# A two-layer encoder trunk on one core: products in couples for nearly all weight panels, with order and memory planned at build time

## Chip, core and metric

The kernel runs on one core of a Trainium2 chip. TensorE (PE) multiplies, VectorE (DVE) and ScalarE (ACT) work element by element, GpSimd (POOL) does small work and issues some DMAs, SyncE (SP) issues the other DMAs. The metric is device microseconds for one execution, as the median of several runs.

## What is computed

The input is 256 rows of 2048 float32 values. Layer 1 is causal softmax attention with 16 heads of 128 and a bias from cumulated forget gates, then a squared-ReLU MLP with 8192 hidden values. From its result come keys and values that layer 2 shares; layer 2 has queries of its own, attention over chunks with a learned bias by distance, and a second MLP. With only 256 rows, the time lies in the products of 256 rows with weights.

```python
h = x
u = rms_norm(h, a_norm_g)
q, k, v, fz = split(u @ a_w_in)                 # 2048 x (3*2048 + 16)
q, k = head_norm(q), head_norm(k)
h = h + forgetting_attention(q, k, v, log_sigmoid(fz + b_f)) @ a_w_out
h = h + relu(rms_norm(h) @ w1[0])**2 @ w2[0]    # 2048 x 8192, 8192 x 2048
k_sh, v_sh = split(rms_norm(h, kv_norm_g) @ kv_w)
q = head_norm(rms_norm(h, b_norm_g) @ b_w_q)
h = h + chunked_relbias_attention(q, head_norm(k_sh), v_sh) @ b_w_out
h = h + relu(rms_norm(h) @ w1[1])**2 @ w2[1]
```

All is float32.

## The kernel before

**Panels and units.** Weights are cut into panels of 512 columns and 2048 rows (16 blocks of 128 rows). There are 96: 12 of `w_in`, 4 of each output projection, 16 up and 16 down of each MLP, 4 of the second query, 8 of `kv`. A panel's weights come in 8 units of two blocks (512 KB). The rows of the result, 256, are two blocks `b`, each with a PSUM bank of its own.

**Three passes.** For precision each operand is split in a high part, rounded to `float32r`, and a low part, the rest. `issue` (L213 on) does it for weights: ScalarE writes `hi` (L227), VectorE `lo` (L228). `passes` (L485 on) then multiplies high by high (L491), low activations by high weights (L493), high activations by low weights (L495). A panel takes 2 x 16 x 3 = 96 matmuls of 512 columns.

**Couples.** Two panels side by side form a pair, and in a pair two row blocks of weights make, with two row blocks of the result, a product of 2 x 2 by 2 x 2 blocks. It is done with seven block products instead of eight (a form of Strassen's method after Winograd). I call such a place a couple: it saves one block product, three matmuls. The weight blocks of a couple are named 11, 12, 21, 22, and the seven left factors are 11, T3 = 22 + 12, T2 = T3 + 11, T1 = 12 + 11, 21, T4 = T2 + 21, and 22. All couples of a pair lie side by side in one tile, so that one instruction makes one factor for all of them. T3 and T2 are sums on VectorE (`make`, L848); T1 and T4 are made by a DMA from GpSimd that adds weights in HBM to a tile in place (`put`, L854), except in the first pair of an MLP, where VectorE makes them. The activations need four sums of blocks, split in high and low as well (`sums`, L287 to L307; tiles `S` and `Sh`). Between the forms ScalarE and VectorE move partial results between PSUM banks (L937, L939, L944, L950, L962).

Pairs with couples are in the MLPs and the second query only: 2 couples in the first up pair of a layer, 3 in the other seven (`WIDE1`), 4 in each of the eight down pairs (`WIDE2`), 2 in each of the two query pairs. The rest of a pair's weights, and all other panels, run as plain units.

**Order.** An MLP goes in four chunks of 2048 hidden values: two up pairs, two down pairs. `Pair.plan` lists forms `f`, `h` and units `a` (first panel) and `b` (second); the last three units of a pair's second panel are left over and run between the first forms of the next pair. Work other than the products is queued by hand in `fill`, a list with one slot for each unit of weights; `run_fill` empties one slot after each. `prepare` starts a pair's weights so many units ahead as the tuple `when` says. Weights come on SP's queue with 4 KB a row (`raw`, four buffers), or 6 or 8 KB for the tiles of couples; split units have three buffers. `keep_order` (L39) fixes the written order on VectorE, ScalarE, TensorE and SP.

**Turns.** Activations must have their columns on the partitions for the next product. `blocks32` (L338 on) transposes blocks of 32 x 32 on VectorE into `z`; then the blocks change places, either by `carry` (L344 to L359), which writes `z` to HBM and reads it back in four DMAs on SP, or by `hop` (L361 to L369), with 16 DMAs from SBUF to SBUF, 8 on SP and 8 on POOL. Only the fourth hidden panel of a chunk uses `hop`.

**Attention.** `attend` gives each head of a group of four its slots: scores, softmax, a `carry` of the probabilities, values. In stage one panels run one after the other, q, k, v of group 0, then of group 1 and so on; in the `kv` stage k and v of each group.

## Time and profile before

| what | us |
| --- | --- |
| median of 3 runs | 2097.28 |
| lowest and highest | 2096.98, 2098.1 |
| the profiled execution's own span | 2090.4 |

The span runs from the first to the last instruction of the profiled execution; the median of the runs counts 6.9 us more around it. Lines of the profile give a source line, an engine, an operation with its tiles (out<-in), a count, busy time and the mean of one in ns, then the engine's idle time before these instructions and what ended it. PEld is the loading of the stationary operand, which runs beside the matmuls. Time stamps are us from the span's start.

### The profile page before, as it was taken

Reading aid. Unit: us, or ns where it says so; the run is one execution under the profiler, and the core shown is the slowest. Engines: PE = TensorE matmul, PEld = TensorE weight load, DVE = VectorE, ACT = ScalarE, POOL = GpSimd, SP = SyncE. Lnnn points to the kernel's source line nnn. Section 1 sums busy time; section 2 is a strip of 40 time slices with the busy share of each in tenths; the row PEclk is TensorE's granted clock in tenths of the full one; section 3 lists DMA queues with packets and bytes.
Section 4 is the critical chain, followed back from the end, with each engine's and each line's share of the span. In section 5 each row is a group of like instructions: output and inputs, shape, how many; then the busy total and the mean of one; then the engine's idle time right before and its main releaser. Section 6 shows DMA issues by size and latency. Waiting matters only on the chain.

```text
span 2090.4 us, 26489 instructions
## 1 busy us (share of the span) xinstructions
PE 2076.3 (99%) x9182; PEld 1709.6 (82%) x9182; DVE 1679.5 (80%) x1972; ACT 1288.4 (62%) x1613; POOL 150.1 (7%) x195
## 2 busy tenths in 40 slices
PE   9999999999999999999999999999999999999999
PEld 7888888878887887887878888888788788878877
DVE  5767666889789889889988577778988897898886
ACT  6544454767567667667776445556765675676674
POOL 1111000001001001001011001000010010010010
PEclk9999999999999999999999999999999999999999
DMA  7777778789689789788878777787987986897885
GB/s 285 248 253 240 232 255 264 250 268 296 232 292 283 241 270 298 231 273 287 280 252 269 233 232 234 247 264 266 294 280 233 284 284 232 291 286 237 274 279 182
DMA packets 176151, 545.14 MB, mean 261 GB/s; under 512 B 37760, under 2 KB 70416, under 8 KB 163728
## 3 DMA queue, kind: packets, MB, share of 16 engines
q1 hardware_dynamic: 163088, 477.31, 64.4%
q0 software_dynamic: 12640, 65.57, 16.2%
q8 instruction: 72, 1.18, 0.2%
q14 instruction: 63, 0.52, 0.1%
q10 hardware_dynamic: 288, 0.57, 0.1%
HBM read 503.49 MB, written 35.68 MB: 258 GB/s over the span
## 4 chain that ended last, share of the span: by engine, by line
PE 86%; DVE 5%; DMA 5%; ACT 2%; issue 2%; SPq 1%; ACTq 0%; DVEq 0%
PE acc L491 22%; PE acc L493 22%; PE acc L495 22%; PE s L495 6%; PE s L491 5%; PE s L493 5%; DVE lo L228 3%; DMA turn<-z 2%; DMA raw<-in_w1sa 1%; ACT hi L227 1%; PE s L635 1%; PE po L665 1%; DVE z L341 1%; DMA raw<-in_w1sb 1%; SPq L357 0%
## 5 line engine op out<-in xcount | busy, mean ns | idle before, releaser
L228 DVE TENSOR_TENSOR lo<-raw,hi 128x1024 fp32r<-128x1024 f32 (+1 forms) x542 | 655.2, 1214 | 189.3 <-ACT hi L227 176.1
L227 ACT ACTIVATE hi<-raw 128x1024 fp32r<-128x1024 f32 (+1 forms) x542 | 569.3, 1053 | 311.3 <-PE acc L493 232.4
L491 PE MATMUL acc<-hi,act 128*128 128x512 f32 x2092 | 580.4, 394 | 1.3 <-ACT hi L227 1.3
L495 PE MATMUL acc<-lo,act 128*128 128x512 f32 x2092 | 571.6, 390 | 0.0
L493 PE MATMUL acc<-hi,act 128*128 128x512 f32 x2092 | 571.0, 389 | 0.1
L493 PEld LDWEIGHTS acc<-hi,act 128*128 128x128 f32 x2092 | 392.7, 188 | 83.0 <-DVE act L321 0.7
L495 PEld LDWEIGHTS acc<-lo,act 128*128 128x128 f32 x2092 | 391.3, 188 | 84.6 <-DVE lo L228 3.4
L491 PEld LDWEIGHTS acc<-hi,act 128*128 128x128 f32 x2092 | 390.5, 188 | 82.0 <-ACT hi L227 3.2
L227 ACT ACTIVATE hi<-w 128x1024 fp32r<-128x1024 f32 x202 | 212.7, 1057 | 93.4 <-PE acc L493 42.9
L228 DVE TENSOR_TENSOR lo<-w,hi 128x1024 fp32r<-128x1024 f32 x202 | 245.5, 1219 | 22.4 <-ACT hi L227 19.1
L228 DVE TENSOR_TENSOR lo<-wT,hi 128x1024 fp32r<-128x1024 f32 x142 | 172.2, 1221 | 60.8 <-ACT hi L227 59.1
L227 ACT ACTIVATE hi<-wT 128x1024 fp32r<-128x1024 f32 x142 | 148.1, 1055 | 74.4 <-PE acc L493 32.2
L495 PE MATMUL s<-lo,act 128*128 128x512 f32 x370 | 102.1, 392 | 6.0 <-DVE lo L228 6.0
L491 PE MATMUL s<-hi,act 128*128 128x512 f32 x370 | 101.1, 390 | 0.0
L493 PE MATMUL s<-hi,act 128*128 128x512 f32 x370 | 100.9, 389 | 0.0
L495 PEld LDWEIGHTS s<-lo,act 128*128 128x128 f32 x370 | 68.7, 188 | 23.8 <-DVE lo L228 10.1
L493 PEld LDWEIGHTS s<-hi,act 128*128 128x128 f32 x370 | 69.5, 188 | 14.4
L491 PEld LDWEIGHTS s<-hi,act 128*128 128x128 f32 x370 | 69.3, 188 | 14.5 <-ACT hi L227 0.3
L848 DVE TENSOR_TENSOR wT<-wT,w 128x1024 f32<-128x1024 f32 (+1 forms) x48 | 66.3, 1381 | 1.6
L668 ACT ACTIVATE act<-po 128x256 fp32r<-128x256 f32 x32 | 12.3, 385 | 88.0 <-PE po L666 88.0
L848 DVE TENSOR_TENSOR wT<-w,w 128x1024 f32<-128x1024 f32 (+1 forms) x48 | 65.5, 1364 | 0.3 <-DMA w<-in_w2fa 0.3
L577 POOL TENSOR_TENSOR ss<-ss,mhalf 128x4 f32<-128x4 f32 x32 | 43.5, 1367 | 271.8 <-DVE ss L576 271.8
(209 smaller groups left out, 1968.8 us busy)
## 6 DMA issues: line engine op xcount, KB each, us to landing
raw<-in_w_in SPq DMA_DIRECT2D x95, 512.0 KB, 4.6
raw<-in_w1sa SPq DMA_DIRECT2D x70, 512.0 KB, 6.4
raw<-in_w1sb SPq DMA_DIRECT2D x70, 512.0 KB, 6.1
w<-in_w2fa SPq DMA_DIRECT2D x32, 1024.0 KB, 7.7
raw<-in_w2sa SPq DMA_DIRECT2D x64, 512.0 KB, 8.0
raw<-in_w_kv SPq DMA_DIRECT2D x64, 512.0 KB, 4.7
w<-in_w2fb SPq DMA_DIRECT2D x32, 1024.0 KB, 7.5
raw<-in_w2sb SPq DMA_DIRECT2D x64, 512.0 KB, 7.3
```

The source lines that it names most:

```text
L227: S.activation(hi[:, c], raw[:, c], AF.Copy)
L228: V.tensor_tensor(lo[:, c], raw[:, c], hi[:, c].bitcast(F32), op=ALU.subtract)
L341: V.transpose(z.rearrange("p (j n b c) -> p b n j c", j=4, n=n, b=nb)[:, b], src.rearrange("p (n j c) -> p n j c", n=n, j=4))
L491: TE.matmul(ps[:, cols], xh, cut(hi, j), start=first, stop=False, **kw)
L493: TE.matmul(ps[:, cols], xl, cut(hi, j), start=False, stop=False, **kw)
L495: TE.matmul(ps[:, cols], xh, cut(lo, j), start=False, stop=last, **kw)
L577: G.tensor_tensor(rn, vv, mhalf, op=ALU.pow)
L635: TE.matmul(s[:, P : 3 * P], q[:, a, P:T], k[:, a], start=True, stop=True)
L665: TE.matmul(po[:, :T], v[:, 0, a * P : (a + 1) * P], pT[:, :2], start=True, stop=False)
L668: S.activation(o[i][:, 0], po[:, :T], AF.Copy)
L848: V.tensor_tensor(d, a, b, op=ALU.add)
```

## The change

The file is written anew around a planner, while the arithmetic of a pair stays.

- **Couples in 47 of 48 pairs.** `pair_list` lists the pairs of all stages. `w_in` is paired too: (q0, k0), (v0, q1), (k1, v1), (q2, k2), (v2, q3), (k3, v3); `kv` as (k, v) of each group; both output projections. Couples: 2 in each pair of `w_in` but the first, which has none, 2 in output projections, query and `kv`, 4 in all pairs of the MLPs. T1 and T4 are made by adding DMAs everywhere.
- **Recorded operations.** Nothing is issued while the code runs through the stages. `K.op` records an operation with its engine, an estimated duration, the cells of 128 columns that it reads and writes, and, for a DMA, the transfer time. Dependencies follow from the cells.
- **Planned order.** `deadlines` goes backward from the products, whose order is fixed, and gives each operation a latest start. `schedule` then runs a simulation of the five engines and the DMA: each engine takes the ready operation with the earliest deadline; TensorE takes ready small work first, else the next product; SP only the first in line. `early` keeps a load or a split from starting more than so many us ahead (22 for weights of the first three blocks, 16 for 21 and units, 9 for splits). The simulated order is then issued, and `order_engines` fixes it on all five engines, POOL's too.
- **Planned memory.** Two arenas in SBUF (71 grains of 256 columns for weights and work, 130 for split operands) are given out during the simulation in grains, which come free when their last reader has ended. PSUM: six banks for panels, two for the rest.
- **One stream of weights.** All weights lie in one array `ws` in the order of use; units come two by two, 1 MB with 8 KB a row; blocks of four couples too have 8 KB a row, blocks of two 4 KB.
- **Turns.** All turns of activations use `hop`; only the probabilities still use `carry`.
- **Smaller.** The gate runs in two passes of 16 matmuls with 256 columns; the halving of the first split and of the last unit is gone.

```diff
-AHEAD = 2
-EARLY = 3
-WIDE = UN + 512
-DEEP = 2 * UN
-WIDE1 = (1, 2, 3, 4, 5, 6, 7)
-WIDE2 = (0, 1, 2, 3, 4, 5, 6, 7)
+CELL = 128
+GRAIN = 256
+ROOM = {"sb": 71, "op": 130}
+MM = 0.22667
+NAMES = ("11", "T3", "T2", "T1", "21", "T4", "22")
+
+IN_C, OUT_C, UP_C, DOWN_C, Q_C, KV_C = 2, 2, (4, 4), (4, 4), 2, 2
+
+def orders(c):
+    m = 8 - c
+    keep = min(3, m)
+    a = [("a", u) for u in range(c, 8)]
+    b = [("b", u) for u in range(c, 8)]
+    tail, b = b[m - keep :], b[: m - keep]
...
+    F = [("f", i) for i in range(7)]
+    plan = [F[0], "r", F[1], "r", F[2], "r", F[3]]
+    left = []
+    for i in range(m):
+        left += a[i : i + 1] + b[i : i + 1]
...
+    cuts = {2: (1, 1, 1), 3: (1, 1, 1), 4: (1, 1, 1), 5: (1, 1, 1), 6: (1, 1, 0)}[c]
+    for i, k in enumerate(cuts):
+        plan += left[at : at + k] + [F[4 + i]]
+        at += k
+    return plan + left[at:], tail
...
+    def deadlines(self, start=11.0, margin=1.0):
+        for o in reversed(self.ops):
+            if o.main:
+                o.ls = o.nominal + start
+                continue
+            ls = 1e9 if o.due is None else o.due
+            for s in o.succ:
+                ls = min(ls, s.ls - (0 if s.eng == o.eng and not o.xfer else self.AFTER[o.eng]) - (margin if s.main else 0.0))
+            o.ls = ls - self.cost(o)
...
+                busy[e] = now + o.dur
+                if o.xfer:
+                    dma = max(now + o.dur + 1.8, dma) + o.xfer
+                    o.end = dma + 1.3
+                    heapq.heappush(events, (now + o.dur, 1, -1, "wake"))
+                else:
+                    o.end = now + o.dur
...
+def dv(n):
+    return 0.07 + 0.00104 * n
...
+    def load(buf, a, b, off, w, at, early, q="Y"):
+        eng = {"Y": SY, "S": S}[q]
+        op(q, 0.45, lambda: eng.dma_start(buf.ap(a, b), flat(off, w, at, at + b - a)), w=[(buf, a, b)],
+           xfer=xfer(P * (b - a) * 4, (b - a) * 4), early=early, name="load")
+
+    def plus(buf, a, b, off, w, at):
+        op("G", 0.87, lambda: G.dma_start(buf.ap(a, b), flat(off, w, at, at + b - a), accum_op=ALU.add),
+           r=[(buf, a, b)], w=[(buf, a, b)], xfer=2.0 * P * (b - a) * 4 / 0.39e6, name="plus")
+
+    def split(buf, a, b, early=9.0):
+        hi, lo = opd("hi", b - a), opd("lo", b - a)
+        op("S", da(b - a), lambda: S.activation(hi.f(), buf.ap(a, b), AF.Copy), r=[(buf, a, b)], w=[hi], early=early, name="hi", hold=[lo])
+        op("V", dv(b - a), lambda: V.tensor_tensor(lo.f(), buf.ap(a, b), hi.ap(), op=ALU.subtract), r=[(buf, a, b), hi], w=[lo], name="lo")
+        return (hi, 0), (lo, 0)
...
+                for b, i in ((b12, "12"), (b22, "22"), (b11, "11")):
+                    load(b, 0, w, *self.src[i], 0, 22)
+                self.form[0] = [split(b11, a, b) for a, b in cuts]
...
+                add(bt, b22, b12, "T3")
+                self.form[1] = [split(bt, a, b) for a, b in cuts]
+                add(bt, bt, b11, "T2")
+                if self.adds:
+                    for a, b in cuts:
+                        plus(b12, a, b, *self.src["11"], a)
...
+                self.form[2] = [split(bt, a, b) for a, b in cuts]
+                self.form[3] = [split(b12, a, b) for a, b in cuts]
+                load(b21, 0, w, *self.src["21"], 0, 16)
+                if self.adds > 1:
+                    self.form[4] = [split(b21, a, b) for a, b in cuts]
+                    for a, b in cuts:
+                        plus(bt, a, b, *self.src["21"], a)
...
+                self.form[5] = [split(bt, a, b) for a, b in cuts]
+                self.form[6] = [split(b22, a, b) for a, b in cuts]
+            for j, (off, us) in enumerate(self.loads):
+                raw = Buf("raw", UN * len(us))
...
+                    load(raw, 0, UN * len(us), off, UN * len(us), 0, 16)
+                for i, u in enumerate(us):
+                    self.unit[u] = split(raw, i * UN, i * UN + UN)
...
+        op("Y", 3.4, lambda: go(SY, 0), r=[z], w=[dst], group=tag, xfer=1.0, name="hop")
+        op("G", 4.0, lambda: go(G, 1), r=[z], w=[dst], group=tag, xfer=1.0, name="hop")
...
+    order = K.schedule()
+    for o_ in order:
+        o_.fn()
+    order_engines(tc, (V.engine, S.engine, TE.engine, SY.engine, G.engine))
```

1773 lines of the change are left out of this document (913 added, 860 removed).

## The prediction

> **What bounds the kernel now.** I read the page first: span, share of each engine, clock, chain.
>
> ```profile
> span 2090.4 us, 26489 instructions
> PE 2076.3 (99%) x9182; PEld 1709.6 (82%) x9182; DVE 1679.5 (80%) x1972; ACT 1288.4 (62%) x1613; POOL 150.1 (7%) x195
> PEclk9999999999999999999999999999999999999999
> PE 86%; DVE 5%; DMA 5%; ACT 2%; issue 2%; SPq 1%; ACTq 0%; DVEq 0%
> ```
>
> TensorE is busy for 99% and makes up 86% of the chain. Busy time of pipelined matmuls is not work at full rate, so next comes the timeline of TensorE: the first product, and two units of weights one after the other in the first stage.
>
> ```profile
> 7.39 1.22 PE L491 MATMUL acc<-hi,act 128*128 128x512 f32 x2 [1.28 <-ACT hi L227]
> ...
> 17.15 1.07 PE L491 MATMUL acc<-hi,act 128*128 128x512 f32 x4
> ...
> 19.87 1.07 PE L491 MATMUL acc<-hi,act 128*128 128x512 f32 x4
> ```
>
> A unit is 12 matmuls of 512 columns and takes 19.87 - 17.15 = 2.72 us, 0.2267 us each; this pitch is the price of a matmul here. The work is 96 panels of 96 matmuls; a couple saves one product of three matmuls. From the code before: up pairs 2 + 7 x 3 = 23 couples a layer, down pairs 8 x 4 = 32, the query 2 x 2, so 2 x 55 + 4 = 114. That leaves 9216 - 342 = 8874 matmuls, 2011.4 us. (With warming, gate, heads, small ones and the six that are halved it gives the page's 9182.)
>
> The attention heads come on top; the timeline in the second attention stage:
>
> ```profile
> 1204.40 1.27 PE L491 MATMUL acc<-hi,act 128*128 128x512 f32 x4
> ...
> 1212.77 0.59 PE L665 MATMUL po<-pbuf,v 128*128 128x256 f32 x2
> ...
> 1213.42 0.39 PE L634 MATMUL s<-k,q 128*128 128x128 f32 x2
> ...
> 1213.89 1.28 PE L491 MATMUL acc<-hi,act 128*128 128x512 f32 x4
> ```
>
> Between the two L491 rows lie three units (8.16 us) and the products of one head: 9.49 - 8.16 = 1.33 us, 42.6 us for 32 heads. The gate's 16 matmuls are 3.6 us, the rest some 0.7: 46.9 in all. And the end:
>
> ```profile
> 2085.82 0.40 PE L495 MATMUL acc<-lo,act 128*128 128x256 f32 x2
> ...
> 2086.26 0.88 DVE L613 SCALAR_TENSOR_TENSOR h<-acc,qn,h 128x256 f32<-128x256 f32 x2 [0.68 <-PE acc L495]
> ```
>
> TensorE ends at 2086.2, 4.2 us before the span does. So 7.4 + 2011.4 + 46.9 + 4.2 = 2069.9, and 20.5 us of the span are TensorE waiting. 1.6 of them lie at the start (36 matmuls from 7.39 to 17.15, 9.76 us against 8.16). Where are the others? Windows over one chunk of the first MLP, and over the second attention stage:
>
> ```profile
> 612.00:779.00 167.00, 166.06 (x730) 136.13 (x729) 142.42 (x145) 107.99 (x121) 10.89 (x16) 1.00 0.84 268
> ...
> 1195.00:1380.00 185.00, 185.00 (x850) 154.46 (x849) 131.44 (x231) 90.04 (x149) 11.49 (x12) 1.00 0.74 239
> ```
>
> Columns: window, length, busy us and count of PE, PEld, DVE, ACT, POOL, clock, DMA share, GB/s. At the pitch 167 us hold 736.7 matmuls; 730 ran: 1.5 us lost in a chunk. The attention stage loses nothing. The chain and TensorE's timeline show the chunk's loss, where the up pairs give way to the down pairs:
>
> ```profile
> 601.47 7.60 DMA turn<-z
> ...
> 611.54 7.46 DMA raw<-in_w1sa
> 619.11 1.06 ACT hi L227
> ...
> 629.59 0.73 PE L495 MATMUL s<-lo,act 128*128 128x512 f32 x2 [0.88 <-DVE lo L228]
> ```
>
> SP sits behind the round trip through HBM, issues the weights after it, and some 10 us later TensorE waits for a low half from VectorE. **TensorE's stream is the bound, with 20 us of gaps.** The span stands 6.9 us below the median of 2097.28.
>
> **What the couples take away.** Counted from the new list of 48 pairs: in 5 x 2, out 4 x 2, up and down 32 x 4, query 2 x 2, kv 4 x 2: 10 + 8 + 128 + 4 + 8 = 158 couples. 44 more remove 132 matmuls, 132 x 0.2267 = **29.9 us**, and leave 8742, 1981.5 us. All lie in the stream, so all count as long as nothing else is late.
>
> The Trainium skill, "TensorE: Matmul & The Clock Gate", Back-to-back issue gap, gives about 131 ns sustained for such a load-and-multiply pair and 215.7 ns isolated; by these the saving would be 17.3 or 28.5 us. The trace's pitch in full stretches is 226.7 ns, so the measured price stands.
>
> **What they add on VectorE and ScalarE.** Groups of the lines view (busy us, mean ns), and one back-to-back pair of the timeline:
>
> ```profile
> L228 DVE TENSOR_TENSOR lo<-raw,hi 128x1024 fp32r<-128x1024 f32 x538 | 652.6, 1218 | 188.3 <-ACT hi L227 175.1 <-PE acc L493 9.3 <-PE s L493 0.7
> L228 DVE TENSOR_TENSOR loh<-w,hih 128x512 fp32r<-128x512 f32 x56 | 38.5, 687 | 8.6 <-ACT hih L227 8.5
> L848 DVE TENSOR_TENSOR wT<-wT,w 128x1024 f32<-128x1024 f32 x34 | 41.7, 1225 | 1.2
> L848 DVE TENSOR_TENSOR wT<-wT,w 128x1536 f32<-128x1536 f32 x14 | 24.6, 1759 | 0.5
> L939 DVE SCALAR_TENSOR_TENSOR acc<-s,p 128x512 f32<-128x512 f32 x17 | 11.8, 695 | 0.0
> L296 DVE TENSOR_TENSOR sum<-q 128x256 f32<-128x256 f32 x16 | 6.7, 419 | 0.0
> L227 ACT ACTIVATE hi<-raw 128x1024 fp32r<-128x1024 f32 x538 | 567.0, 1056 | 310.4 <-PE acc L493 232.4 <-PE s L493 31.6 <-DMA raw<-in_w_in 13.5
> ...
> 614.84 2.35 DVE L228 TENSOR_TENSOR lo<-raw,hi 128x1024 fp32r<-128x1024 f32 x2
> ```
>
> - Splits: a pair with c couples splits 16384 + 1536c columns (seven forms of 512c, 8 - c units of 1024 in either panel). In tiles of 1024 that is 939 before and 1005 after; with the 98 halves of before at 0.687, VectorE gains 1005 x 1.218 - 1147 = 77 us, ScalarE 66 x 1.056 = 70.
> - Sums of weights (T3, T2): 1024 columns a couple, 158 x 1.225 = 193 against 142 before: 51 us. T1 and T4 now always come by an adding DMA.
> - Moves between banks: 47 pairs with couples instead of 34, 13 x 2 x 0.695 = 18 us; ScalarE 23.
> - Sums of activations: 25 sets instead of 21, some 10 us (a set is 4 x 0.419 + 1.218).
>
> VectorE: 1679.5 + 156 = 1836 us, 89% of 2055; ScalarE some 67%. In an MLP chunk VectorE has 142.4 of 167 us now; it gets 2.5 for splits (88 tiles against 78 and 14 halves) and 2.7 for sums, 148 of 4 x 180 x 0.2267 = 163.2, or 90%. The pair above begins its second tile 1.13 us after the first, so these busy times overcount a little. I cost all of it at nothing: TensorE covers it. Without cover, in a chunk where VectorE lags by a tile at each boundary, it would be 1.2 us a chunk, within the 1.5 below.
>
> **Turning through hops.** All 60 turns of activations (24 panels outside the MLPs' hidden ones, 32 hidden, 4 between the layers) now go straight from SBUF to SBUF, 8 DMAs on SP and 8 on POOL. Before, only the last panel of each hidden chunk does; the trace of one:
>
> ```profile
> 646.47 1.31 DVE L341 STREAM_TRANSPOSE z<-acc 128x512 f32<-128x512 f32 x2
> ...
> 647.81 5.38 SPq L367 DMA_DIRECT2D q<-z  x8
> ...
> 657.52 1.04 ACT L871 ACTIVATE q<-q 128x1024 f32<-128x1024 f32 x1
> ...
> 661.58 1.23 DVE L882 TENSOR_TENSOR act<-q,act 128x1024 fp32r<-128x1024 f32 x1 [0.82 <-ACT q L878]
> ```
>
> From the block transposes to the finished low half are 16.3 us. In the new order the third hidden panel is wanted at unit a4 of the down pair, behind four forms of c = 4 and three left-over units, 7 x 2.72 = 19 us after the up pair ends. It fits by 2.7 us. The price is 60 x 5.4 = 323 us of SP, in which no weights are issued; weights are planned 16 to 22 us ahead, which hides a hop if the arena has room. Per chunk I take 0.5 us lost, between nothing and the 1.5 of now; eight chunks, 4 us.
>
> **Last heads before the output projection.** k and v of group 3 now end in one pair: k at its end, v three units into the next. That pair wants heads 12 and 13 at a6: seven forms of 1.36, three left-over units and seven own, 36.7 us after k; heads 14 and 15 at a7, 39.4. Turning k needs the norm and the hop, some 16 us by the rows above and this one (two of them):
>
> ```profile
> L577 POOL TENSOR_TENSOR ss<-ss,mhalf 128x4 f32<-128x4 f32 x32 | 43.5, 1367 | 271.8 <-DVE ss L576 271.8
> ...
> 309.25 0.38 PE L634 MATMUL s<-k,q 128*128 128x128 f32 x2
> ...
> 334.15 0.38 PE L666 MATMUL po<-pbuf,v 128*128 128x128 f32 x2
> ```
>
> The last head of stage one takes 24.9 us from scores to values, paced by fill slots of one unit. With heads some 3 us apart that gives 16 + 9 + 25 = 50, 10 us late; without slots there is no lateness. I take 4, nearer to no slots since nothing there is slotted any more; bounds 0 and 10, twice.
>
> **Start, end, DMA.** The first split isn't halved any more: 0.5 us on the 1.6. The last unit is no longer cut by rows, so 0.75 us of residual is added to the 4.2. The DMA queues:
>
> ```profile
> q1 hardware_dynamic: 163088, 477.31, 64.4%
> q0 software_dynamic: 12640, 65.57, 16.2%
> ```
>
> That is 2.82 and 5.16 us of 16 engines per MB. Adding DMAs grow from 110 couples to 158 of 0.524 MB, 25 MB or 130 us; hops instead of round trips save about 27 MB, 77 us, and 8 KB rows some more. The share goes from 81% to at most 84%. I cost it at nothing; loads issued ahead hide it.
>
> **The sum.** 7.4 + 1981.5 + 46.9 + 4.9 = 2040.7, plus waits of 2.1 + 8 + 4 = 14.1: a span of 2054.8, and with the 6.9 around it **2062 us**. So the time is 2047.6 + S with S the waits; S = 49.7 eats everything.
>
> **Rivals.**
> - All hidden: S under 5, about 2050. For it: deep prefetch, an arena in place of three split buffers. Against: a turn that fits by 2.7 us.
> - The plan is late: both head boundaries at 10, chunks at 1.5, so S = 2.1 + 20 + 12 = 34, 2082; with VectorE a tile late as well up to 2093. For it: VectorE at 90% and all five engines in one fixed order, which can't go round a late operation.
> - SP's queue becomes the bound (slower): a hop waits at SP's head for late transposes, and the weights behind it stay unissued, as behind the round trip at 601. If each of the 32 hidden hops costs the 1.5 us that a chunk loses now, 48 more: 2110. It decides from 39 / 32 = 1.2 us a hop. Against it: the hop at 647 delayed nothing that TensorE waited for.
> - POOL's issues are held up by VectorE (slower): 480 hop issues instead of 64. If each waits one tile of 1.2 us, a hop is 8 x 1.2 = 10 us later, the third hidden panel misses a4 by 7 us, 8 times: 2062 + 56 = 2118. Against it, the source view of L367:
>
> ```profile
> L367 POOL DMA_DIRECT2D q<-z x64: 498/498/554, 481.6 to 2019.5; - x64
> ```
>
>   All 64 took 498 to 554 ns beside a VectorE that was 85% busy. The Trainium skill, "SBUF — State Buffer", Who interferes with whom, says that a VectorE operation on two SBUF inputs and a GpSimd operation that reads SBUF lock each other out; by the row, issuing isn't hit.
> - It does not do what it says: TensorE isn't the bound, and fewer products change nothing (within 0.2%). The Trainium skill, "Perfetto Trace Analysis", Identifying the Most-Contended Engine, judges TensorE by its weight loads, 82% here, which would leave 18% room. Against it: the weight load
>
> ```profile
> L493 PEld LDWEIGHTS acc<-hi,act 128*128 128x128 f32 x2092 | 392.7, 188 | 83.0 <-DVE act L321 0.7
> ```
>
>   takes 188 ns of a pitch of 227, 83%, in stretches that wait for nothing: 82% is full here.
>
> **Chances.** Forecast (2053 to 2078) 0.56; all hidden 0.10; late plan (2078 to 2093) 0.14; within 0.2%, which is about what a measurement of this kernel tells from no change, 0.05 (2093 to 2101.5; 0.02 of it the last rival); SP's queue 0.12; POOL 0.03. Faster 0.80, same 0.05, slower 0.15. The range is 2048 to 2093, the first three cases.
>
> **What would show it.** 9060 matmuls in place of 9182 (132 fewer products, 16 more for a gate in two passes, 6 halves fewer). VectorE near 1836 us. In an MLP window of 167 us over 730 matmuls: chunks are better than now. TensorE waiting for values or act of the last heads some 40 us into an output projection: that term. Long SP waits on z with late raw tiles: SP's queue. POOL hop issues over 0.6 us: the lock. I am wrong if TensorE's idle time is well above 35 us, or if the pitch of 0.2267 changes.

## The result, and the profile after

| | before | after |
|---|---|---|
| median of the runs, us | 2097.13 (2093.11 to 2098.1, 4 runs) | 2108.2 (2106.89 to 2110.73, 4 runs) |
| ratio, 95% interval | 1 | 1.0056 (1.0042 to 1.007) |
| profiled execution: span, us | 2090.4 | 2107.1 (its time 2108.88) |
| mean granted clock of TensorE | 1.000 | 0.992 |

The change makes the kernel 0.56% slower. I had forecast 2062 us, 1.7% faster. The page of the changed kernel, span, busy times and DMA queues:

```profile
span 2107.1 us, 27585 instructions
PE 2056.4 (98%) x9060; PEld 1695.7 (80%) x9060; DVE 1804.9 (86%) x2062; ACT 1364.1 (65%) x1658; POOL 438.6 (21%) x701
q1 hardware_dynamic: 108608, 436.93, 56.1%
q0 software_dynamic: 39296, 103.88, 25.3%
```

TensorE runs the 9060 matmuls that were forecast and is busy for 19.9 us less, but the span is 16.7 us longer: TensorE waits more. Which wait? TensorE's list of waits, first the kernel before (waiting line, what released it, total us, times, longest):

```profile
PE s L495 <- DVE lo L228: 7.0, 10, 0.9
PE acc L491 <- ACT hi L227: 1.3, 1, 1.3
PE pt L92 <- DVE mhalf L94: 1.1, 1, 1.1
```

and the changed one:

```profile
PE ps L489 <- ACT ps L574: 18.1, 10, 5.0
PE ps L489 <- ACT arena_op L469: 10.6, 3, 7.6
PE ps L836 <- DMA arena_sb<-arena_sb: 4.6, 2, 2.5
PE ps L491 <- DVE arena_op L1081: 3.8, 3, 2.5
PE ps L869 <- DMA arena_sb<-turn: 3.7, 3, 1.4
PE ps L495 <- DVE arena_op L470: 2.0, 1, 2.0
```

L469 and L470 are the two halves of a split, L574 is the second of ScalarE's two copies between the banks behind a pair's second form, L836 the scores, waiting for a hop, L869 the values, waiting for turned probabilities. These are 42.8 us in place of 9.4; no releaser has half of them, and single waits are up to 7.6 us long where none was over 1.3.

Behind the longer waits stands something else. Windows of the changed kernel (length, busy us and count of PE, PEld, DVE, ACT, POOL, then granted clock, DMA share, GB/s):

```profile
7.90:18.00 10.10, 5.00 (x12) 3.95 (x13) 7.67 (x8) 8.04 (x13) 0.00 (x0) 0.50 1.01 420
233.20:236.50 3.30, 3.30 (x9) 2.56 (x9) 0.00 (x0) 0.00 (x0) 0.00 (x0) 0.50 1.02 423
834.00:837.30 3.30, 3.30 (x9) 2.56 (x9) 3.09 (x4) 1.06 (x1) 0.20 (x1) 0.51 1.02 264
1055.80:1062.50 6.70, 4.46 (x11) 3.50 (x12) 5.55 (x7) 5.09 (x8) 3.99 (x8) 0.50 0.30 77
1267.40:1270.70 3.30, 3.30 (x10) 2.53 (x9) 3.30 (x4) 2.00 (x2) 0.00 (x0) 0.50 1.10 418
1298.20:1304.90 6.70, 6.04 (x14) 4.79 (x15) 5.20 (x6) 3.07 (x4) 4.34 (x9) 0.50 0.72 231
```

In six stretches the clock is granted at half. TensorE is busy for 25.4 us of them, and half of that, 12.7 us, is lost beside the waits themselves. Before, the record of the clock begins at 10.52 us and shows no such stretch until the last product is done. But ahead of 10.52 the first six products, from 7.39 us on, took 2.73 us, 0.455 each, which is half rate too, so that some 1.4 us were lost in this way before as well:

```profile
10.12 0.81 PE L491 MATMUL acc<-hi,act 128*128 128x512 f32 x2
```

To see where in the work this lies, I cut TensorE's stream into the stages of the model, after the number of full-size products that each has, and take from each stage's length its products at 0.2267 us. What is left is the stage's **loss**: waits, slow clock, and the small products of the gate and of the heads (1.33 us a head, 16 heads a layer). In us:

| stage | before | after | difference |
|---|---|---|---|
| until the first product | 7.4 | 13.0 | +5.6 |
| first projection (in) | 22.4 | 30.5 | +8.1 |
| output projection, layer 0 | 5.4 | 8.2 | +2.8 |
| MLP, layer 0 | 8.6 | 15.0 | +6.4 |
| query | 2.1 | 2.5 | +0.4 |
| keys and values (kv) | 14.9 | 37.3 | **+22.4** |
| output projection, layer 1 | 6.8 | 8.0 | +1.2 |
| MLP, layer 1 | 8.5 | 6.1 | -2.4 |
| after the last product | 4.2 | 5.1 | +0.9 |

The sum is +45.4. There are 126 full-size products fewer, 28.6 us. 45.4 - 28.6 = 16.8, the 16.7 of the spans. (The last unit before also has 12 products of half size, counted apart: their 1.4 us lie in the 8.5 of its second MLP.) **The saving came; the waits that came with it are larger.** Half of them are in kv. Timeline of SP's queue there (start, us, line, issues in one row; SP's waits between the issues are in the us of a row):

```profile
1216.31 9.36 SPq L701 DMA_DIRECT2D arena_sb<-turn  x16
1225.78 12.97 SPq L457 DMA_DIRECT2D arena_sb<-in_ws  x3
1238.80 11.15 SPq L686 DMA_DIRECT2D arena_sb<-arena_sb  x16
1250.12 9.44 SPq L457 DMA_DIRECT2D arena_sb<-in_ws  x6
...
1269.22 12.11 SPq L701 DMA_DIRECT2D arena_sb<-turn  x16
...
1282.33 6.82 SPq L686 DMA_DIRECT2D arena_sb<-arena_sb  x8
1289.24 9.14 SPq L457 DMA_DIRECT2D arena_sb<-in_ws  x3
```

What SP waited for, over the whole kernel (us, times, longest), the two lines of the hops:

```profile
SPq L686 <- DVE arena_sb L675: 204.6, 48, 18.0
SPq L686 <- DMA arena_sb<-in_ws: 94.6, 49, 3.8
```

The first are hops that wait for their transposes, the second hops that wait for weights to land. In none of the twenty traces of this case is a DMA issued on SP's or POOL's queue before the eighth before it on that queue has landed. So the last two issues of the hop at 1282 wait for the two loads ahead of it, which land at 1286.9 and 1288.6. The planner's simulation has no such limit. Whether the chip or the program's own semaphores set it, the traces don't show.

ScalarE at the end of this stretch:

```profile
1294.67 1.15 ACT L813 ACTIVATE arena_sb<-arena_sb,gqk 128x1024 f32<-128x1024 f32 x1 [5.33 <-DMA arena_sb<-arena_sb]
1295.73 1.99 ACT L469 ACTIVATE arena_op<-arena_sb 128x1024 fp32r<-128x1024 f32 x2
1297.62 0.58 ACT L573 ACTIVATE arena_sb<-ps 128x512 f32<-128x512 f32 x1
1298.22 0.58 ACT L574 ACTIVATE ps<-ps 128x512 f32<-128x512 f32 x1
```

And TensorE:

```profile
1294.09 1.07 PE L495 MATMUL ps<-arena_op 128*128 128x512 f32 x4
1298.86 1.22 PE L489 MATMUL ps<-arena_op 128*128 128x512 f32 x2 [3.70 <-ACT ps L574]
...
1301.58 1.91 PE L489 MATMUL ps<-arena_op 128*128 128x512 f32 x4
1303.29 1.83 PE L491 MATMUL ps<-arena_op 128*128 128x512 f32 x4
```

SP issues a hop at 1282; it lands at 1294; ScalarE, whose order says that the query comes next, stands for 5.33 us; two splits and two copies that need nothing of the hop stand behind it; TensorE waits 3.7 us for the copies and then runs at 0.43 us a product (1303.29 - 1301.58 = 1.71 for four) where it takes 0.2267 in full clock. SP, ScalarE and TensorE in fixed orders, one late step, and the price is paid by TensorE.

My theories were: **A**, the couples' own steps (splits, sums, copies) crowd stages that already hold heads; **B**, SP's queue of hops and reads holds the weights back; **L**, late steps in a fixed order hold urgent ones; **P**, the planner's prices are too low, so that its plan has no slack. The start is apart.

### The profile page after: what moved, and what is told of

Read it like the earlier page. It is cut to its first block, busy times and chain, and to the rows that moved or that the text cites. A ratio compares the mean times of both kernels' runs of the same rounds, so it can differ in the third digit from the quotient of the medians.

```text
span 2107.1 us, 27585 instructions
## 1 busy us (share of the span) xinstructions
PE 2056.4 (98%) x9060; PEld 1695.7 (80%) x9060; DVE 1804.9 (86%) x2062; ACT 1364.1 (65%) x1658; POOL 438.6 (21%) x701
## 3 DMA queue, kind: packets, MB, share of 16 engines
q0 software_dynamic: 39296, 103.88, 25.3%
## 5 line engine op out<-in xcount | busy, mean ns | idle before, releaser
L469 ACT ACTIVATE arena_op<-arena_sb 128x1024 fp32r<-128x1024 f32 x1005 | 1026.1, 1054 | 552.8 <-PE ps L491 300.9
L470 DVE TENSOR_TENSOR arena_op<-arena_sb,arena_op 128x1024 fp32r<-128x1024 f32 x1005 | 1192.5, 1219 | 175.0 <-ACT arena_op L469 159.2
L489 PE MATMUL ps<-arena_op 128*128 128x512 f32 x2914 | 836.2, 394 | 29.6 <-ACT ps L574 18.1
L491 PE MATMUL ps<-arena_op 128*128 128x512 f32 x2914 | 830.0, 392 | 3.8 <-DVE arena_op L1081 3.8
L495 PE MATMUL ps<-arena_op 128*128 128x512 f32 x2914 | 831.1, 392 | 2.0 <-DVE arena_op L470 2.0
L489 PEld LDWEIGHTS ps<-arena_op 128*128 128x128 f32 x2914 | 548.7, 189 | 150.9 <-ACT ps L574 23.8
L491 PEld LDWEIGHTS ps<-arena_op 128*128 128x128 f32 x2914 | 550.0, 189 | 120.8 <-DVE arena_op L1081 5.4
L495 PEld LDWEIGHTS ps<-arena_op 128*128 128x128 f32 x2914 | 547.4, 189 | 115.3 <-DVE arena_op L470 2.4
L461 POOL DMA_DIRECT2D arena_sb<-in_ws x158 | 139.4, 882 | 1070.2 <-DVE arena_sb L526 589.3
L686 POOL DMA_DIRECT2D arena_sb<-arena_sb x480 | 240.6, 520 | 383.4 <-DVE arena_sb L675 96.1
L526 DVE TENSOR_TENSOR arena_sb<-arena_sb 128x1024 f32<-128x1024 f32 x158 | 192.5, 1222 | 15.5 <-DMA arena_sb<-in_ws 12.7
L719 DVE SCALAR_TENSOR_TENSOR h<-ps,smalls,h 128x512 f32<-128x512 f32 (+1 forms) x65 | 46.5, 738 | 18.8 <-PE ps L495 18.8
L675 DVE STREAM_TRANSPOSE arena_sb<-ps 128x512 f32<-128x512 f32 x64 | 43.5, 701 | 16.9 <-DMA arena_sb<-in_ws 8.0
L1071 ACT ACTIVATE arena_sb<-arena_sb 128x1024 f32<-128x1024 f32 x32 | 33.8, 1055 | 32.4 <-DMA arena_sb<-arena_sb 13.9
L1081 DVE TENSOR_TENSOR arena_op<-arena_sb,arena_op 128x1024 fp32r<-128x1024 f32 x32 | 39.1, 1222 | 14.2 <-ACT arena_sb L1075 14.2
L675 DVE STREAM_TRANSPOSE arena_sb<-arena_sb 128x512 f32<-128x512 f32 (+1 forms) x64 | 40.8, 642 | 2.3 <-ACT arena_sb L813 0.4
L579 ACT ACTIVATE ps<-ps 128x512 f32<-128x512 f32 x47 | 27.4, 582 | 18.8 <-DVE arena_sb L675 14.1
L656 ACT ACTIVATE arena_op<-arena_sb 128x1024 fp32r<-128x1024 f32 x25 | 26.4, 1054 | 19.5 <-DVE arena_sb L654 18.5
L1074 ACT ACTIVATE arena_op<-arena_sb 128x1024 fp32r<-128x1024 f32 x32 | 34.0, 1061 | 0.9
```

Of the source, the lines that this page charges most:

```text
L461: op("G", 0.87, lambda: G.dma_start(buf.ap(a, b), flat(off, w, at, at + b - a), accum_op=ALU.add), r=[(buf, a, b)], w=[(buf, a, b)], xfer= ...
L469: op("S", da(b - a), lambda: S.activation(hi.f(), buf.ap(a, b), AF.Copy), r=[(buf, a, b)], w=[hi], early=early, name="hi", hold=[lo])
L470: op("V", dv(b - a), lambda: V.tensor_tensor(lo.f(), buf.ap(a, b), hi.ap(), op=ALU.subtract), r=[(buf, a, b), hi], w=[lo], name="lo")
L489: TE.matmul(ps.ap(), x(xh), cut(hi, j), start=first, stop=False, skip_group_check=True)
L491: TE.matmul(ps.ap(), x(xl), cut(hi, j), start=False, stop=False, skip_group_check=True)
L495: TE.matmul(ps.ap(), x(xh), cut(lo, j), start=False, stop=last, skip_group_check=True)
```

## Experiments

A caution for reading them: the planner plans the whole kernel, so that an edit in one stage moves steps in every other. The loss by stage tells more than the total, and four experiments keep the plan as it is. Each loss is that of one execution, the profiled one; most lie within 7 us of their kernel's median, but that of the heads over DRAM is 8.6 us above it and that with all prices but VectorE's 8.8 us below. The kernel before, run beside these on the same chips, had medians of 2095.0 to 2095.7 us, each from 11 to 21 runs, and each ratio is to that. The changed kernel was not run again beside them, so a difference of 2 or 3 us from its 2108.2 is not told apart from that between chips.

### One suspect at a time, planned anew

**The first tile taken as landed sooner.**

```diff
-           xfer=xfer(P * (b - a) * 4, (b - a) * 4), early=early, name="load")
+           xfer=xfer(P * (b - a) * 4, (b - a) * 4) if q == "Y" else 0.01, early=early, name="load")
```

> One change: the planner takes the first weight tile (the one issued from ScalarE's queue) as landed at once, so its split stands first among the weight splits on ScalarE. If the order of ScalarE is what makes the first product start at 12.99 us where it started at 7.39 before, the first product starts at 7 to 8.5 us and the run takes 4 to 8 us less than the changed kernel's 2108 (5 of the wait, up to 2.5 of the half clock after it). If the landing of the loads is what holds it (more loads in flight than before), it stays at 12 to 13 us and the run at 2108, give or take 3 for what a new plan moves elsewhere.

2099.95 us (2093.71 to 2107.92, 10 runs; ratio to before 1.0025, 1.001 to 1.004). The total fell as forecast, but not for the reason: the first product started at 11.54 us, 1.5 sooner, as I read the code because the planner's model of a single DMA channel still puts this tile behind the others. kv lost 22.4 us in place of 37.3 with its couples and hops untouched. **So 15 us of kv's loss can come or go by the plan alone.**

**kv without couples.**

```diff
-IN_C, OUT_C, UP_C, DOWN_C, Q_C, KV_C = 2, 2, (4, 4), (4, 4), 2, 2
+IN_C, OUT_C, UP_C, DOWN_C, Q_C, KV_C = 2, 2, (4, 4), (4, 4), 2, 0
```

> One change: the four panel pairs of the shared key and value projection have no couples, as before the change. That adds 24 full-size products, 5.4 us of TensorE. Theory A, the couples' own needs (their splits, sums and copies, crowded with the heads and the probabilities) make that stage lose 37.3 us where it lost 14.9: the stage falls back to about 15, and the run to about 2108 - 22 + 5 = 2091. Theory B, SP's queue of hops and probability reads makes the loss whatever the weights are: the stage keeps at least 30 us and the run is at 2108 to 2114.

2106.96 us (2103.32 to 2108.83; ratio 1.0051, 1.0032 to 1.007). kv fell to 20.3, near the 15 of A, for 5.4 us of products; but A's 2091 did not come: the second MLP now lost 13.6 in place of 6.1, and the total hardly moved.

**Heads turned over DRAM.**

```diff
-            hop(z, dst)
+            carry(z, dst)
             if then:
```

> One change: the normed heads are turned by one write to DRAM and four reads on SP (as the probabilities are) in place of 8 issues on SP and 8 on POOL. That takes about 3 us of SP for each of the 16 heads that are turned and normed. Theory B (SP's queue holds the weights): the losses of the in stage (30.5 us) and of the key and value stage (37.3) fall together by 12 to 25 us, and the run to 2083 to 2096. Theory A (the couples' own needs): within 4 us of 2108. If the way over DRAM lands later than the hop did, the scores wait for it and the run is longer than 2108.

2114.61 us (2106.3 to 2123.25; ratio 1.0077, 1.0047 to 1.0106), slower; but the reason named for that, the scores' waits for turned heads, is 1.8 us only. By the stages of its profiled execution, which took 2123.25, kv fell to 26.6 and in to 26.0, 15 us together, as B has it; the output projection of layer 0 rose to 14.5 and the MLPs to 21.7 and 23.4, though no MLP has such a head.

**SP's prices** (theory P).

```diff
-        op("Y", 3.4, lambda: go(SY, 0), r=[z], w=[dst], group=tag, xfer=1.0, name="hop")
+        op("Y", 5.4, lambda: go(SY, 0), r=[z], w=[dst], group=tag, xfer=1.0, name="hop")
...
-        op("Y", 1.8, reads, r=[box], w=[dst], xfer=xfer(P * z.n * 4, n * 4), name="back")
+        op("Y", 2.4, reads, r=[box], w=[dst], xfer=xfer(P * z.n * 4, n * 4), name="back")
```

> No change of the work: only the planner's prices for two of SP's steps are set to what the trace shows (a hop 5.4 us in place of 3.4, the four reads of probabilities 2.4 in place of 1.8). If the loss is a plan that reckons SP too cheap, so that weights stand behind hops that last longer than planned, the plan moves the weights ahead and the run is 5 to 20 us under 2108. If SP's capacity or the late operations themselves make it, the run stays within 4 us of 2108.

2106.46 us (2103.17 to 2112.3; ratio 1.0055, 1.0035 to 1.0074): no gain, kv at 36.6. SP's price alone isn't it.

### The plan kept, single steps moved

These use a function that moves a step ahead in the planned order, past every step with which it shares neither an operand nor memory (`lies` gives the memory of a step):

```diff
+    def ahead(o, far):
+        at = order.index(o)
+        mine, j = lies(o), at
+        while j and far(order[j - 1]) and order[j - 1] not in o.deps and not any(
+                s == t and a < d and c < b for s, a, b in mine for t, c, d in lies(order[j - 1])):
+            j -= 1
+        order.insert(j, order.pop(at))
...
```

**Copies ahead of late steps.** (The two copies get the name `p7`.)

```diff
+    for o_ in [o for o in order if o.name == "p7"]:
+        ahead(o_, lambda x: x.name != "p7")
```

> The plan of the changed kernel is kept as it is, with its memory and the order of TensorE, VectorE, SP and POOL; only ScalarE's two copies behind each pair's second form (the saved bank and the negated bank) are moved ahead of the splits and other late steps that stand before them in ScalarE's order, as far as their operands allow. Theory L (late steps in ScalarE's fixed order hold these copies): TensorE's 18.1 us of waits for the copies fall below 6, the half clock behind the longest of them goes, and the run is 10 to 20 us under 2108. Rival (the copies are late because the form itself is, or the splits that they pass are as urgent): TensorE waits as long for the splits, and the run is within 4 us of 2108.

2105.21 us (2102.7 to 2106.39; ratio 1.0048, 1.0032 to 1.0064). Waits of the moved kernel:

```profile
PE ps L489 <- ACT ps L574: 10.2, 5, 4.7
PE ps L836 <- DMA arena_sb<-arena_sb: 7.5, 3, 3.7
```

The copies' waits fell from 18.1 to 10.2 (ten to five) and the scores' waits for hops rose from 4.6 to 7.5. Of eighteen microseconds three were won, or 1.7 by the ratios to the kernel before. Theory L had expected the copies' waits under 6: it is right about a part of the place and wrong about the worth.

**The first split in front.**

```diff
+    main_ = [o for o in order if o.main][:2]
+    keep_ = main_[0].deps | main_[1].deps
+    for o_ in [o for o in order if o in keep_ and o.name in ("hi", "lo")]:
+        ahead(o_, lambda x: x not in keep_)
```

> The plan is kept; only the two halves of the first weight tile's split are moved to the front of the splits on ScalarE and VectorE. Theory: the tile itself lands near 7 us (5.7 us after its issue at 1.2), so the first product starts at 8 to 8.7 us in place of 12.99, the half clock at the start is as long or shorter, and the run is 4 to 7 us under 2108. If the landing holds it, it stays at 11 us or more and the run gains under 2.

2110.52 us (2103.74 to 2114.99; ratio 1.0074, 1.0056 to 1.0093): no gain. Timeline of TensorE in this kernel:

```profile
10.06 2.04 PE L489 MATMUL ps<-arena_op 128*128 128x512 f32 x4 [3.95 <-ACT arena_op L469]
11.89 1.85 PE L491 MATMUL ps<-arena_op 128*128 128x512 f32 x4
16.46 1.67 PE L495 MATMUL ps<-arena_op 128*128 128x512 f32 x4 [2.72 <-DVE arena_op L470]
```

The first product came 2.9 us sooner, the third group of four then waited for a low half, and the in stage ended at 297.8 us, where it ended before the move.

**Both, with a longer warm-up.** (The two moves above, and this.)

```diff
-        for _ in range(11):
+        for _ in range(18):
```

> Both moves together, and 18 warm-up products in place of 11, so that TensorE is busy until the first product can start; the plan is kept. If the half clock at the start comes from TensorE's idle time between the warm-up and the first product (7.6 us), there is none before the first long wait, which is worth another 1.5 to 3.5 us. If the parts add, the run is 16 to 28 us under 2108: 2080 to 2092, which is under the kernel before (2095). If it is at 2100 or above, what the moves win is lost again behind them.

2106.36 us (2101.84 to 2111.98; ratio 1.0055, 1.0038 to 1.0071). The first product started at 8.56, 4.4 sooner, and no half clock stood ahead of it. The in stage then lost 40.3 us in place of 30.5; in the whole kernel the scores waited 12.6 us for hops, in place of 4.6. What was won at the head of a fixed order was spent at its next late step.

**The warm-up alone.** (29 products in place of 11.)

> The changed kernel and its plan; only the warm-up has 29 products in place of 11, so that TensorE is busy until the first product at about 13 us. If its idle time of 7.6 us is what halves the clock there, no half clock stands in the record before the first later wait, and the first 12 products of the first unit take 2.7 us in place of about 5. The in stage then comes to the next tile earlier; if the tiles' landing sets the pace there, the run stays within 2 us of 2108, else it gains 2 to 5.

2108.43 us (2103.65 to 2112.78; ratio 1.0058, 1.004 to 1.0077). Timeline of TensorE:

```profile
1.05 9.19 PE L450 MATMUL ps<-arena_sb 128*128 128x128 f32 x58 [1.05 <-DVE mhalf L444]
12.99 2.06 PE L489 MATMUL ps<-arena_op 128*128 128x512 f32 x4 [2.75 <-ACT arena_op L469]
...
17.44 1.09 PE L489 MATMUL ps<-arena_op 128*128 128x512 f32 x4
```

I had the warm-up too short: it ran faster once the clock was full and left a wait of 2.75 us, which was enough to halve the clock again, for 3.41 us in place of 10.24. The first twelve products took 4.45 us, up to 17.44. With the short warm-up, in the changed kernel:

```profile
12.99 2.07 PE L489 MATMUL ps<-arena_op 128*128 128x512 f32 x4 [7.63 <-ACT arena_op L469]
...
18.19 1.08 PE L489 MATMUL ps<-arena_op 128*128 128x512 f32 x4
```

they took 5.2. So idle time does halve the clock; at the start it is worth 0.8 us here, and the total doesn't show it.

### The planner's prices

**All prices as the trace has them.** The group of VectorE's halves in the changed kernel:

```profile
L470 DVE TENSOR_TENSOR arena_op<-arena_sb,arena_op 128x1024 fp32r<-128x1024 f32 x1005 | 1192.5, 1219 | 175.0 <-ACT arena_op L469 159.2
```

1.219 us each, where the planner reckons 0.07 + 0.00104 x 1024 = 1.135. The steps on 512 columns are as much too cheap, 0.08 us on most of 2062 steps.

```diff
 def dv(n):
-    return 0.07 + 0.00104 * n
+    return 0.155 + 0.00104 * n
 def da(n):
-    return max(0.07 + 0.00086 * n, 0.21 + 0.00078 * n)
+    return max(0.07 + 0.00086 * n, 0.24 + 0.0008 * n)
...
-        op("V", 0.66, go, r=[ps, acc] + ([r2()] if r2 else []), w=[acc], name="res")
+        op("V", 0.74, go, r=[ps, acc] + ([r2()] if r2 else []), w=[acc], name="res")
```

VectorE's other steps on 512 columns go to 0.70 or 0.71, ScalarE's 0.95 to 1.06 (the query's scale 1.15), SP's as above.

> No change of the work: the planner's prices of VectorE's, ScalarE's and SP's steps are set to the durations of the trace (a 1024-column step on VectorE 1.22 us in place of 1.13, a 512-column one 0.70 to 0.74 in place of 0.60 to 0.66, a 1024-column step on ScalarE 1.06 in place of 0.95 to 1.01, a hop on SP 5.4 in place of 3.4). The plan holds VectorE to be some 80 % busy where it is 86 %. If the waits come from a plan that runs ahead of the engines, the total of TensorE's waits falls by half (from about 45 us to under 25) and the run is 10 to 25 us under 2108. If they come from what no price shows (landing times of the loads, the order itself), the run stays within 5 us of 2108.

2104.3 us (2100.36 to 2107.19; ratio 1.0044, 1.0028 to 1.0059). By the total the second half of the expectation held: the run is 3.9 us under 2108, and TensorE's waits are 41.7 us in place of 45.4, not halved. The total hides a finding: the MLPs lost 3.2 and 4.0 us where they lost 15.0 and 6.1, and no wait for L574 stands in its list of waits. It isn't this plan alone: in all eight kernels with these prices the two MLPs together lost 6.5 to 15.6 us, in the seven plans without them, or with a part of them, 20 to 45. But kv lost 41.9 and the output projection behind it 16.5. There, two hops stood in one row on SP, by its timeline:

```profile
1207.82 3.01 SPq L457 DMA_DIRECT2D arena_sb<-in_ws  x6
1210.89 16.75 SPq L686 DMA_DIRECT2D arena_sb<-arena_sb  x16
```

TensorE beside it:

```profile
1221.66 0.73 PE L489 MATMUL ps<-arena_op 128*128 128x512 f32 x2 [2.38 <-ACT arena_op L469]
...
1229.37 0.77 PE L836 MATMUL ps<-arena_sb 128*128 128x128 f32 x2 [6.50 <-DMA arena_sb<-arena_sb]
```

Of the 16.75 us, 9.3 are the 16 issues. In the rest SP waits, five times, for the loads ahead of them to land; over the whole kernel:

```profile
SPq L686 <- DMA arena_sb<-in_ws: 104.4, 52, 4.4
```

The scores wait 6.5 us for the second of the two hops. With the MLPs free of noise, the two suspects of kv could be asked again.

**Re-priced plan, heads over DRAM** (this edit and the one of the heads above).

> The kernel with the re-priced plan (2104.3 us), whose MLP stages lose next to nothing and whose key and value stage loses 41.9 us, and in it one change: the 16 normed heads are turned by one write to DRAM and four reads on SP in place of a hop of 8 issues on SP and 8 on POOL. Theory B (SP's queue of hops makes the loss of the stages with heads): the in stage and the key and value stage together fall from 69 us of loss to 45 or less, and the run to 2070 to 2085. Theory A (the couples' own steps on VectorE and ScalarE, crowded with the heads): these two stages stay above 60 us, and the run at 2098 or more.

**Re-priced plan, kv without couples** (`KV_C` is 0 as above).

> The kernel with the re-priced plan (2104.3 us), and in it the four panel pairs of the shared key and value projection without couples (24 more products, 5.4 us). Theory A: that stage's loss falls from 41.9 us to 15 to 20 and that of the output stage behind it from 16.5 to about 8, so the run is at 2104 + 5 - 24 - 8 = 2077, say 2072 to 2088, and under the kernel before (2095). Theory B: the stage's loss stays above 35 and the run is at 2105 to 2112.

| loss, us | before | after | re-priced | and heads over DRAM | and kv plain |
|---|---|---|---|---|---|
| first product | 7.4 | 13.0 | 13.1 | 13.4 | 13.2 |
| in | 22.4 | 30.5 | 27.1 | 25.3 | 25.9 |
| output, layer 0 | 5.4 | 8.2 | 8.8 | 17.6 | 8.9 |
| MLP, layer 0 | 8.6 | 15.0 | 3.2 | 2.0 | 2.7 |
| kv | 14.9 | 37.3 | 41.9 | 19.1 | 16.3 |
| output, layer 1 | 6.8 | 8.0 | 16.5 | 12.6 | 13.4 |
| MLP, layer 1 | 8.5 | 6.1 | 4.0 | 5.8 | 4.1 |
| median, us | 2095.0 | 2108.2 | 2104.3 | 2084.03 | **2080.07** |
| ratio to before | | 1.0056 | 1.0044 | 0.9953 (0.9937 to 0.9969) | 0.993 (0.9911 to 0.995) |

Both cures bring kv down, each alone: with its heads over DRAM it lost 19.1, without couples 16.3. Neither A nor B is the cause by itself. Over all experiments kv lost 16.3 to 23.8 us in the six plans without its couples, 19.1 to 26.6 in the three with heads over DRAM and couples, and 22.4 to 41.9 in the nine kernels with hops and couples both. **With heads, hops and couples together the stage mostly loses much more, but not always: the plan with the first tile taken as landed sooner holds all three at 22.4.** So the plan decides under this load; which step of it costs the stage is not shown, and a window tells only that VectorE has more to do. A window over the stage, re-priced with couples:

```profile
1128.00:1338.00 210.00, 193.25 (x840) 158.08 (x839) 157.79 (x242) 110.34 (x168) 47.34 (x69) 0.95 0.69 216
```

and re-priced with kv plain:

```profile
1127.00:1317.00 190.00, 190.00 (x864) 158.26 (x863) 137.49 (x219) 96.88 (x149) 38.04 (x60) 1.00 0.66 223
```

The plain stage runs 24 matmuls more in 20 us less, with TensorE never idle and the clock full; VectorE has 20 us less to do. And this kernel is under both, the one before and the changed one.

**And the first projection without couples too** (`IN_C` is 0 as well).

> As the one before, and the five panel pairs of the first projection that have couples are without them too (54 more products than the changed kernel in all, 12.2 us of TensorE). If the couples of the first projection lose as much as they save, this run is equal to the one before within 3 us (the in stage falls from 27 us of loss to about 20, for 6.8 us of products). If they lose more than they save, it is faster by over 3 us; if less, slower by over 3.

2085.24 us (2083.31 to 2087.66; ratio 0.9949, 0.9932 to 0.9967), 5.2 slower. There the couples earn most of their 6.8 us, though that stage has heads and hops as well. What saves it isn't shown; its couples are 10 in 6 pairs, kv's 8 in 4.

**The first loads in single tiles,** and the first split in front:

```diff
-                    load(raw, 0, UN * len(us), off, UN * len(us), 0, 16)
+                    for i in range(len(us) if self.n == 0 and j < 3 else 1):
+                        a, b = (i * UN, i * UN + UN) if self.n == 0 and j < 3 else (0, UN * len(us))
+                        load(raw, a, b, off, UN * len(us), a, 16)
```

> The kernel with the re-priced plan (2104.3 us), and in it the first pair's first three loads in pieces of one tile (512 KB, 4 KB rows) in place of two (1 MB, 8 KB rows), and the first tile's split at the front of ScalarE's. Theory: the start is late because the two-tile loads land together and late; the first product then starts at 7.5 to 9 us in place of 13.1, the third to tenth products follow without waits over 1.5 us, and the in stage's end comes 3 to 6 us sooner, the run at 2098 to 2101. Rival: the in stage's end is set by waits behind the start (heads, hops, late weights), so that its end moves by under 1.5 us and the run is at 2103 to 2106.

2094.07 us (2088.54 to 2100.64, 11 runs; ratio 0.9992, 0.9979 to 1.0004). The first product started at 8.27 us and the in stage ended at 290.6 where the re-priced one ended at 294.5. The run is under both halves of the expectation. The rest of the 10 us is what the new plan moved elsewhere: kv lost 30.1 in place of 41.9 and the output projection behind it 9.6 in place of 16.5, while the first output projection lost 5 us more and the MLPs 8. As with the first split in front, TensorE then waited for a low half, 2.69 us at 13.5, so not all of the start was won.

### Which price, and do the parts add?

The edits of the re-pricing were split, with kv plain in both: `dv` and VectorE's constants alone, then all the others without them.

> Key and value stage without couples, and only VectorE's prices in the planner set to the durations of the trace; ScalarE's and SP's as in the change. All prices gave 2080 on this base, none 2107. If VectorE's are what matters (its 1022 products' halves and 2062 steps at 0.08 us too little each), the run is at 2078 to 2086 and the MLP stages lose under 5 us each; if the hop's price on SP matters as well, it stays above 2092.

> Key and value stage without couples; ScalarE's and SP's prices in the planner set to the durations of the trace, VectorE's as in the change. All prices gave 2080 on this base, VectorE's alone 2104, none 2107. If ScalarE's and SP's are what matters, the run is at 2079 to 2086. If the plan holds only where every price is right, it stays at 2096 or more, with TensorE waiting for VectorE's halves or for copies behind them.

On the base with plain kv: no price changed 2107.0, VectorE's alone 2103.75 (2099.36 to 2109.39, 10 runs), all but VectorE's 2095.49 (2086.65 to 2104.64, 11 runs), all 2080.07. Both second halves of these expectations held, the second but for half a microsecond (its edge was 2096): with VectorE's alone, TensorE waited ten times for L469 and nine times for L470; without VectorE's, the second MLP lost 13.6 us. Neither set does it: with no price, VectorE's, the others and all, the two MLPs lose some 30, 21, 20 and 7 us. The kernel with all but VectorE's also has the widest spread of all, 18 us.

Then edits shown above were put together, on the re-priced plan: first single tiles at the start, heads over DRAM and plain kv; the same with couples in kv; and single tiles and plain kv with the hops as they were.

> Re-priced plan, first loads in single tiles with the first split in front, normed heads turned over DRAM, and no couples in the key and value stage. If the parts are separate microseconds, this is the 2080 of the kernel with re-priced plan and plain key and value stage less about 4 for the start and 0 to 5 for the hops: 2070 to 2077. If they are the same microseconds (either the hops or the couples had to go), only the start's 4 come: 2075 to 2081.

> The same with couples kept in all pairs of panels but one, as in the change: 5.4 us fewer products than the run beside it. If the hops over DRAM free the key and value stage as far as plain weights do, it is 3 to 6 us faster than that run; if the couples crowd the heads even so, it is slower by 2 to 10.

> The fastest version (re-priced plan, key and value stage without couples, 2080), and in it the first pair's first three loads in single tiles and the first split in front. If the start's microseconds are its own, the first product starts at 8.2 us in place of 13.2 and the run is at 2074 to 2078. If the in stage's end is set by what stands behind the start, or the new plan loses as much elsewhere, it is at 2079 to 2088.

| re-priced plan, kv plain, and: | median, us | ratio to before |
|---|---|---|
| nothing else | 2080.07 | 0.993 (0.9911 to 0.995) |
| start in single tiles | 2080.22 | 0.9925 (0.9912 to 0.9938) |
| start, heads over DRAM | 2089.3 | 0.9968 (0.9957 to 0.9978) |
| start, heads over DRAM, kv with couples | 2089.45 | 0.9964 (0.995 to 0.9978) |

The parts don't add: the first halves of all three expectations failed, and the two runs with heads over DRAM lie outside the second halves too. With the heads' hops gone, couples still cost kv something there (25.9 us of loss with them, 16.7 without). With single tiles the first product started 5.0 us sooner (8.2), yet the in stage ended at 293.0 where it ended at 293.4. With heads over DRAM both output projections lost 16 to 17 us, since the last values waited for VectorE and for turned probabilities.

## Why the prediction was wrong

The sum was 2040.7 + S, with the waits S at 14.1. The span of 2107.1 gives S = 66.4.

- **Products, pitch, forms: right.** 9060 matmuls, as worked out. The pitch stayed, as a window over the first MLP of the re-priced kernel shows:

```profile
387.00:1043.00 656.00, 654.08 (x2882) 540.35 (x2881) 588.72 (x585) 452.64 (x488) 132.49 (x217) 1.00 0.88 271
```

  656.0 / 2882 = 0.2276 us a product, with the waits in it and VectorE at 90%. What 44 couples more save is real, and the best version has 36 of them.
- **VectorE: 1804.9 us where I had 1836,** ScalarE 65% where I had 67%: 31 us too much, no matter for the result.
- **The step that failed: "I cost all of it at nothing: TensorE covers it",** and with it that the attention stages lose nothing but 8 us at their ends. By stage, less the small products that I had counted (24.9 and 21.3 us), S is 5.6 at the start (I had 2.1), 21.1 in the MLPs (4), 2.5 in the query (nothing), 13.8 in the first projection with the output projection behind it, and 24.0 in kv with its own (8 for both). The price of a tile (1.22 us) was right and VectorE's share (86%) no bound by itself. But cover has to be there at each place, and the order is fixed on all engines. In the MLPs the missing cover cost 21.1 - 7.2 = 13.9 us, shown by the re-priced plan, which does the same work. In kv 22.4 came on. Taking the couples or the hops of the heads away brings most of it back, but so did one plan that kept both; so both the load and the plan's order bear on it, and the single step behind it stays open.
- **"Weights are planned 16 to 22 us ahead, which hides a hop": right in the MLPs, wrong in kv.** I multiplied hops by 5.4 us of SP and never asked how many stand in one row. In kv two stand in a row (11.15 us in the changed kernel, 16.75 in the re-priced one), beside rows of 16 reads of 9.36 and 12.11 us. Nor did I ask what a hop waits for at SP: it can't be issued to its end before the loads ahead of it have landed.
- **Chunks at 4 us together, head boundaries at 8:** the 4 were for all waits in the chunks, and the MLPs lost 21.1 us, five times that (before, 17.1 with the 1.4 of the half-size products). 5.0 of them are a single wait for L574 at the boundary to the query; the slow clock behind it makes 2.2 of the query's 2.5. In 560 to 727 us the window holds 732 matmuls, over the 730 that I named; in the next one 718. With true prices the MLPs lost 7.2, so the term was near for a plan that holds. The output projections rose by 4.0 together, so the boundaries were not too cheap; the terms for in (+8.1) and kv (+22.4) were missing. I had written that the attention stage loses nothing before, and took it to stay so.
- **Start at 2.1 us:** it costs 5.6 until the first product and more behind it. I took half a microsecond off for the split and didn't look at the loads: two tiles in one DMA land together.
- **The clock:** no term at all. 12.7 us, against some 1.4 before; those are most of the 1.6 that I found at the start and took for waits.
- **The rivals.** SP's queue gave 2110, by chance the measured time: its mechanism is there at the heads, while for the 32 hidden hops, where I had put its 48 us, TensorE's list has 3.8 us (L1081). The sign that I named, SP waiting for transposes, is in its list (204.6 us), but SP waited 170 us for them before as well, and 119 for the round trips. The lock between VectorE and POOL is refuted by the hop's line, seen by its source (ns, least, median, longest; first and last start):

```profile
L686 POOL DMA_DIRECT2D arena_sb<-arena_sb x480: 496/498/823, 60.0 to 2035.5; - x160
L686 SPq DMA_DIRECT2D arena_sb<-arena_sb x480: 507/588/2272, 74.6 to 2041.4; - x160
```

  POOL's issues take 0.498 us, as before (the longest 0.823); SP's up to 2.27.
  That TensorE isn't the bound is refuted as well: 36 couples more than before, in the re-priced plan with kv plain, give 0.7%.
- **Outside the span** I added 6.9 us; the changed kernel has 1.8. The profiled execution of before was a fast one of its spread (2090.5 to 2102.7 in the later runs), so 5 us of my forecast were no cost of anything.

What stays open: why the in stage bears its couples and kv mostly doesn't; and what a plan that knows of the eight DMAs in flight would lose, since no experiment gave the planner that limit. The half clock is not the main part of kv's loss: by the windows above it is half of 3.30 + 6.04 us, 4.7 of 37.3.

## What to carry to other kernels

Where every engine runs a fixed order, a share of busy time says nothing on cover: count, stage by stage, how long steps stand in one row on each queue, what they wait for there, and what urgent step lies behind them. Set a planner's prices to the durations of a trace before judging a change by its total, all of them together. And take one stage's loss, not the total, as the result of an experiment that plans anew.

## What I had not expected of the hardware

How short a wait halves the clock. In the profiles of the changed kernel, the re-priced one, its two cures of kv and the one with the warm-up of 29 products, no half clock begins behind a wait of TensorE under 1.89 us; of 17 waits from 1.89 to 2.55 us 9 have one, and all from 2.75 us up. The other profiles have exceptions, such as these: behind waits of 3.66 us (the first split in front) and 2.83 us (the copies ahead) none begins, behind one of 1.80 us (kv without couples, not re-priced) one does. It lasts 3.41, 6.83 or 10.24 us, whole steps of 3.41. The Trainium skill, "TensorE: Matmul & The Clock Gate", What's actually happening, gives a free-running window of 3413 ns, and the trace's steps agree; its section HAM oscillation — how this bites in real kernels warns of idle gaps over some 3.4 us, while in the changed kernel

```profile
833.45 1.75 PE L491 MATMUL ps<-arena_op 128*128 128x512 f32 x4 [2.50 <-DVE arena_op L1081]
```

2.50 us were enough for the half clock of the window at 834.0 above; the measurement decides. So a wait of 2.5 us can cost, by my estimate, its 2.5 and, with TensorE busy in a window of 3.41 us at half rate, 1.7 more.
